# Block transpositions on VectorE and small fetches for retention's v, k and y, with y normalized on ScalarE

## The chip, the cores and the metric
The kernel runs on one core of a Trainium2 chip. A core has several engines, each with its own instruction stream in program order: TensorE (PE in the profile, matmuls), VectorE (DVE), ScalarE (ACT), GpSimd (POOL) and SyncE (SP), which here issues most DMA transfers. Engines wait for one another by semaphores. The metric is the device time of one launch in microseconds (us), lower is better.

## The reference, cut to what matters
One layer: an RMSNorm, an input projection, two groups of heads (retention and windowed attention), a gate, an output projection, a residual and a last RMSNorm. Sequence 1024, model width 2048, all float32.

```python
def hybrid_layer(x, w_in, w_out, norm_w, decay_fwd, decay_bwd, gn_w, gn_b, sink):
    h = rms_norm(x, norm_w)
    proj = h @ w_in                                  # (1024, 2048) @ (2048, 6656)
    rq, rk, rv, rg, aq, ak, av, ag = jnp.split(proj, splits, axis=-1)
    y_ret = retention_branch(rq, rk, rv, decay_fwd, decay_bwd, gn_w, gn_b) * jax.nn.silu(rg)
    y_att = window_attention_branch(aq, ak, av, sink) * jax.nn.silu(ag)
    return x + jnp.concatenate([y_ret, y_att], axis=-1) @ w_out

def retention_chunkwise(q, k, v, log_gamma, include_diag):   # chunks of 128 rows, 8 heads of 128
    scores = jnp.einsum('bhnik,bhnjk->bhnij', qc, kc) * decay
    inner = jnp.einsum('bhnij,bhnjv->bhniv', scores, vc)
    kv_chunk = jnp.einsum('bhnjk,hj,bhnjv->nbhkv', kc, k_dec, vc)
    _, prev = lax.scan(lambda s, kv: (s * chunk_decay + kv, s), zeros, kv_chunk)
    cross = jnp.einsum('bhnik,hi,nbhkv->bhniv', qc, q_dec, prev)
    return inner + cross

# retention_branch: rotary on q and k, the above forwards and backwards, and then per head
y = (y - mean(y)) * lax.rsqrt(var(y) + GN_EPS) * gn_w + gn_b
```

## The kernel before, in words
The two projections are products of 2x2 blocks in seven multiplications instead of eight (operands a11, a12, a21, a22 of the weights and sums of them). Each float32 operand is split into a high and a low part (`split`: ScalarE writes the high part wH at L87, VectorE the low part wL at L84), and a product is three matmuls, L98, L99 and L100 (`mm3`); L100 uses wL. The projected heads go to DRAM as tiles `pr` of 128x1024, with the head's feature in the partition and the position along the row, that is, the transposed form.

The main loop is a clock of steps. In each step TensorE issues two of the projection's products (six matmuls of 128x512), and beside it jobs, written as Python generators, each put a little work of the other stages: the attention's heads, then the eight retention heads, then the gating and the operands of the output projection. `idle(n)` lets n steps pass, `busy` holds the heads whose y isn't finished. The instructions of TensorE, SP and POOL stand in the order in which the jobs write them; those of VectorE and ScalarE are placed by a scheduler.

A retention head takes 28 steps. `fetch` loads kT and qT and their halves for the rotation (`rx`) by SP and rotates them on VectorE (L751, L753, L91); `fetch_v` loads vT by SP (L761). `head` then does, in order: the scores kT x qT (L787), decayed by VectorE into `sd` (L790); `transposed` turns vT into v_tok on TensorE in two bundles of four 128x128 transpositions (L542), which ScalarE copies out (L797), and kT into k_tok likewise (L803); `vd` is v_tok with its decays; the outer products vd x k_tok (L820) give the state of each chunk, which VectorE scans forwards and backwards (L832, L834) and splits into sH and sL, 14 pieces of 128x128; the inner products v_tok x sd (L867) and the cross products with sH, sL give y (L860, L868). `normed` takes statistics of y on VectorE (L882, L883), has POOL raise the variance to the power -1/2 (L888), normalizes y on VectorE in eight instructions (L891), turns it on TensorE (L542) and lets ScalarE scale it by gn_w and gn_b on the way out of PSUM (L899); SP stores it to `mix` (L905), 128x1024 a head.

Of the DMA queues, SP's carries the weights (`a<-in_w_in`, L171; a tile's next load waits until its last reader is done), the heads' loads and the stores of mix, all in one order. In the gating (`operand_tiles`), ScalarE's own queue loads a tile of mix (L1280) and a tile of the gate (L1281), ScalarE applies Silu (L1270) and VectorE multiplies (L1271). In the attention, two tiles of v are turned by `transposed` as well (`take_v`).

## Time and profile before
| what | us |
|---|---|
| median of 3 runs | 1526.39 (1525.41 to 1526.89) |
| span of the profiled execution | 1524.4 |
| its own time beside its span, by the median of the runs | 1526.39 - 1524.4 = 2.0 |
| TensorE busy | 1510.5 |
| VectorE busy | 1088.3 |
| ScalarE busy | 686.6 |
| POOL busy | 151.0 |

The span is the time from the first to the last instruction of one profiled execution. The busy times of the engines overlap, so they don't add up to it; an engine's share says how much of the span it had something running. The profile also has a chain of work that ended last, groups of instructions by line and shape with the mean duration of one, waits with what ended them, DMA transfers with the time from issue to landing, and a timeline. The eight retention heads run from about 690 to 1110 us, the gating of their part from about 1219 to 1284 us.

### The profile page before, as it was taken

The numbers are of one execution on the slowest core, as the hardware profiler recorded it, in microseconds if no ns is written. First come the engines' busy times: TensorE is split into PE (matmuls) and PEld (weight loads), VectorE is DVE, ScalarE is ACT, GpSimd is POOL, SyncE is SP. The second block draws the span as 40 slices with busy tenths as digits, with TensorE's granted clock in tenths as the row PEclk, the third lists the DMA queues.
The fourth block names the chain that finished last, engine by engine and source line by source line (L and its number), as shares of the span: only waits on it lengthen the run. The fifth ranks groups of instructions, "written<-read, shape, count | busy, mean of one in ns | idle before, by whom it ended". The sixth has DMA issues, their size and how long they took to land.

```text
span 1524.4 us, 20497 instructions
## 1 busy us (share of the span) xinstructions
PE 1510.5 (99%) x7406; PEld 1274.0 (84%) x7406; DVE 1088.3 (71%) x1943; ACT 686.6 (45%) x1139; POOL 151.0 (10%) x169
## 2 busy tenths in 40 slices
PE   9999999999999999999999999999999999999997
PEld 7888888788888888888888888888888888888886
DVE  6896594557767575756977797779755966776766
ACT  7543462234545454533445444543444643542425
POOL 0000001111010000011212000001211102020001
PEclk9999999999999999999999999999999999999999
DMA  8288847889573424796677655488689679395756
GB/s 319 68 277 316 311 166 193 222 207 251 163 204 128 138 80 167 281 315 156 139 179 205 196 174 193 152 297 299 157 207 262 152 217 251 85 212 162 219 177 251
DMA packets 153352, 310.53 MB, mean 204 GB/s; under 512 B 13697, under 2 KB 72481, under 8 KB 144418
## 3 DMA queue, kind: packets, MB, share of 16 engines
q1 hardware_dynamic: 128050, 254.15, 49.1%
q0 software_dynamic: 19728, 36.71, 15.6%
q10 hardware_dynamic: 5472, 18.36, 3.5%
q8 instruction: 58, 0.95, 0.3%
q14 instruction: 44, 0.36, 0.1%
HBM read 193.03 MB, written 124.52 MB: 208 GB/s over the span
## 4 chain that ended last, share of the span: by engine, by line
PE 84%; issue 9%; DMA 4%; DVE 2%; POOL 0%; ACT 0%; SPq 0%; ACTq 0%; POOLq 0%; DVEq 0%
PE pj L100 21%; PE pj L98 21%; PE pj L99 21%; PE ax L99 5%; PE ax L100 5%; PE ax L98 5%; PE ax L820 2%; PE ax L542 1%; DMA xt<-in_x_dram 1%; PE ax L619 1%; DMA pr<-ct 1%; PE ax L787 1%; PE ax L867 1%; DMA yt<-pr 1%; DVE wL L84 0%
## 5 line engine op out<-in xcount | busy, mean ns | idle before, releaser
L98 PE MATMUL pj<-c,wH 128*128 128x512 f32 x1444 | 576.8, 399 | 0.0
L100 PE MATMUL pj<-c,wL 128*128 128x512 f32 x1440 | 562.6, 391 | 1.6 <-DVE wL L84 1.6
L99 PE MATMUL pj<-c,wH 128*128 128x512 f32 x1444 | 563.0, 390 | 0.0
L100 PEld LDWEIGHTS pj<-c,wL 128*128 128x128 f32 x1440 | 270.3, 188 | 60.7 <-DVE wL L84 2.5
L98 PEld LDWEIGHTS pj<-c,wH 128*128 128x128 f32 x1444 | 271.6, 188 | 49.7 <-ACT ct L292 0.4
L99 PEld LDWEIGHTS pj<-c,wH 128*128 128x128 f32 x1444 | 271.8, 188 | 49.5 <-DVE c L948 0.2
L87 ACT CAST wH<-a 128x1024 fp32r<-128x1024 f32 (+1 forms) x159 | 166.3, 1046 | 250.2 <-PE pj L99 138.0
L84 DVE TENSOR_TENSOR wL<-a,wH 128x1024 fp32r<-128x1024 f32 x157 | 191.9, 1222 | 109.4 <-ACT wH L87 105.9
L292 ACT COPY ct<-pj 128x512 f32<-128x512 f32 x192 | 111.1, 584 | 220.3 <-PE pj L100 219.7
L262 POOL DMA_DIRECT2D pr<-ct x104 | 92.2, 961 | 612.9 <-DVE ct L91 474.6
L91 DVE TENSOR_TENSOR ct<-pj,ct 128x512 f32<-128x512 f32 x164 | 109.1, 688 | 58.9 <-PE pj L100 58.0
L84 DVE TENSOR_TENSOR wL<-s,wH 128x1024 fp32r<-128x1024 f32 x56 | 68.4, 1222 | 89.8 <-ACT wH L87 89.4
L99 PE MATMUL pj<-wL,c 128*128 128x512 f32 x224 | 87.3, 390 | 0.0
L100 PE MATMUL pj<-wH,c 128*128 128x512 f32 x224 | 87.2, 389 | 0.0
L98 PE MATMUL pj<-wH,c 128*128 128x512 f32 x224 | 87.1, 389 | 0.0
L99 PE MATMUL ax<-wL,c 128*128 128x512 f32 x208 | 81.2, 390 | 0.4 <-DVE wL L84 0.4
L100 PE MATMUL ax<-wH,c 128*128 128x512 f32 x208 | 80.9, 389 | 0.0
L98 PE MATMUL ax<-wH,c 128*128 128x512 f32 x208 | 80.9, 389 | 0.0
L87 ACT CAST wH<-s 128x1024 fp32r<-128x1024 f32 x56 | 59.1, 1055 | 16.4 <-PE ax L100 8.8
L87 ACT CAST sH<-st 128x128 fp32r<-128x128 f32 x112 | 29.9, 298 | 46.9 <-DVE st L834 29.2
L99 PEld LDWEIGHTS pj<-wL,c 128*128 128x128 f32 x224 | 42.0, 188 | 8.9 <-DVE wL L84 0.3
L98 PEld LDWEIGHTS pj<-wH,c 128*128 128x128 f32 x224 | 42.0, 188 | 8.8
(243 smaller groups left out, 2057.7 us busy)
## 6 DMA issues: line engine op xcount, KB each, us to landing
a<-in_w_in_dram SPq DMA_DIRECT2D x103, 512.0 KB, 5.8
kept<-c SPq DMA_DIRECT2D x28, 1024.0 KB, 7.3
c<-kept SPq DMA_DIRECT2D x28, 1024.0 KB, 9.9
pr<-ct SPq DMA_DIRECT2D x110, 256.0 KB, 5.4
pr<-ct POOLq DMA_DIRECT2D x104, 256.0 KB, 6.2
a<-in_w_out_dram SPq DMA_DIRECT2D x18, 512.0 KB, 5.4
rx<-pr SPq DMA_DIRECT2D x64, 128.0 KB, 3.8
ysrc<-mix ACTq DMA_DIRECT2D x16, 512.0 KB, 5.4
```

The source lines that it names most:

```text
L84: return nc.vector.tensor_tensor(out=dst, in0=src, in1=high.bitcast(F32), op=ALU.subtract)
L87: behind(pinned, nc.scalar.copy(out=dst_h, in_=src))
L91: nc.vector.tensor_tensor(out=dst, in0=a, in1=b, op=ALU.add)
L98: nc.tensor.matmul(po, aH, bH, start=first, stop=False, **kw)
L99: nc.tensor.matmul(po, aH, bL, start=False, stop=False, **kw)
L100: nc.tensor.matmul(po, aL, bH, start=False, stop=last, **kw)
L262: nc.gpsimd.dma_start(out=dst, in_=t, accum_op=ALU.add)
L292: nc.scalar.copy(out=t, in_=bank)
L542: nc.tensor.transpose(pt[:, blk(t)], src[:, blk(b * 4 + t)], ident)
L619: nc.tensor.transpose(pt[:, blk(j)], s[:, blk(j)], ident)
L787: nc.tensor.matmul(sc[:, blk(t)], kT[:, c], qT[:, c], start=True, stop=True)
L820: nc.tensor.matmul(p, k_tok[:, c], vd[:, c, d], start=True, stop=True)
```

## The change
VectorE can transpose the 32x32 blocks inside a tile, each block where it stands. If the blocks themselves are moved to their transposed places by a transfer, the two together turn a 128x128 tile. The change does this for v, k and y of the retention heads and for v of the attention; the function `transposed` and its 208 TensorE instructions are gone.

- **v**: `gather` fetches vT from its plain row tile by 16 transfers of 32x8x32 elements (rows of 32 floats, 128 bytes) on SP instead of one; VectorE transposes two halves of 128x512 into v_tok, straight in SBUF. `fetch_v` lets seven steps pass instead of five.
- **k**: when k is rotated, VectorE also transposes its two halves into `ct` tiles, which SP stores to a DRAM tile `kz` in blocks. A new job `fetch_k_tok`, started at the scores, waits until no y is unfinished, and SP fetches k_tok by four transfers of 32x32x32. The next head's kT is started when k_tok is there, instead of before `vd`.
- **y**: a small VectorE instruction makes -mean x rstd; ScalarE normalizes y by eight instructions with scale and bias; VectorE transposes its two halves into `ct`, and SP stores these to mix in blocks. The scale by gn_w and bias by gn_b moves to the gating, as one more ScalarE instruction on each of eight tiles, which are fetched by four transfers on SP instead of one on ScalarE's queue.
- **state splits**: one split for both directions, 128x2x128, seven a head instead of fourteen; sH and sL are laid out by direction, and the cross products read them with a stride.

```diff
+    def gather(q, dst, src):
+        rows = [dst[a * SQ:(a + 1) * SQ] for a in range(P // SQ)]
+        if len(src.shape) == 3:
+            of = src.rearrange("c (b j) (a t) -> a j (c b) t", j=SQ, t=SQ)
+            for a, r in enumerate(rows):
+                q(out=r.rearrange("p (n t) -> p n t", t=SQ), in_=of[a])
+        else:
+            of = src.rearrange("(b j) (c a t) -> a b j c t", j=SQ, t=SQ, a=P // SQ)
+            for a, r in enumerate(rows):
+                r = r.rearrange("p (c b t) -> b p c t", b=P // SQ, t=SQ)
+                for b in range(P // SQ):
+                    q(out=r[b], in_=of[a, b])
...
+                    if c == T_RK:
+                        zs.append(ct())
+                        nc.vector.transpose(out=zs[i], in_=u)
                     yield
                 kq[name, h] = t
+                for i, z in enumerate(zs):
+                    yield
+                    nc.sync.dma_start(out=spot(kz[h], i), in_=chunks(z))
...
-                nc.sync.dma_start(out=t, in_=pr[T_RV + h])
-                yield from idle(5)
+                gather(nc.sync.dma_start, t, pr[T_RV + h])
+                yield from idle(7)
                 vs[h] = t
+
+            def fetch_k_tok(h):
+                while busy:
+                    yield
+                yield
+                t = ret.tile([P, NT, P], F32, name="k_tok", tag="y")
+                gather(nc.sync.dma_start, t.rearrange("p c e -> p (c e)"), kz[h])
+                yield from idle(6)
+                ks[h] = t
...
-                for b, pt in transposed(vs.pop(h)):
-                    nc.scalar.copy(out=v[:, 4 * b:4 * b + 4], in_=chunks(pt))
+                vT = vs.pop(h)
+                for b in range(2):
+                    nc.vector.transpose(out=v[:, 4 * b:4 * b + 4], in_=chunks(vT[:, half(b)]))
                     yield
-                while busy:
-                    yield
-                k_tok = ret.tile([P, NT, P], F32, name="k_tok", tag="y")
-                for b, pt in transposed(kT):
-                    nc.scalar.copy(out=k_tok[:, 4 * b:4 * b + 4], in_=chunks(pt))
-                    yield
-                start(next_of("kT", T_RK, h + 1))
                 vd = ret.tile([P, NT, 2, P], F32, name="vd", tag="vdq")
                 for d in range(2):
                     nc.scalar.mul(vd[:, :, d], v, kd[:, d * RH + h:d * RH + h + 1])
-                yield from idle(3)
+                while h not in ks:
+                    yield
+                k_tok = ks.pop(h)
+                start(next_of("kT", T_RK, h + 1))
...
-                        split(sH[:, 2 * to + d - 1], sL[:, 2 * to + d - 1], cur[:, d])
                         if d == 1:
+                            both = slice(i, 2 * NT - 2 - i, 2 * NT - 3 - 2 * i)
+                            split(sH[:, both], sL[:, both], cur)
                             prev = cur
...
-                for c in range(NT):
-                    nc.vector.tensor_scalar(out=y[:, c], in0=y[:, c], scalar1=mv[:, c, 0:1], scalar2=rs[:, c:c + 1],
-                                            op0=ALU.subtract, op1=ALU.mult)
+                nc.vector.scalar_tensor_tensor(out=mv[:, :, 0], in0=mv[:, :, 0], scalar=-1.0, in1=rs, op0=ALU.mult, op1=ALU.mult)
+                zs = []
+                for b in range(2):
+                    for c in range(4 * b, 4 * b + 4):
+                        nc.scalar.activation(out=y[:, c], in_=y[:, c], func=AF.Identity, scale=rs[:, c:c + 1], bias=mv[:, c, 0:1])
+                    zs.append(ct())
+                    nc.vector.transpose(out=chunks(zs[b]), in_=y[:, 4 * b:4 * b + 4])
+                    yield
+                busy.discard(h)
                 yield from idle(2)
-                outs = []
-                for b, pt in transposed(y.rearrange("p c e -> p (c e)")):
-                    yo = ct()
-                    nc.scalar.activation(out=yo, in_=pt, func=AF.Identity, scale=gw[:, h:h + 1], bias=gb[:, h:h + 1])
-                    outs.append((mix[h][:, half(b)], yo))
-                    yield
-                busy.discard(h)
-                yield
-                for dst, yo in outs:
-                    nc.sync.dma_start(out=dst, in_=yo)
+                for b, z in enumerate(zs):
+                    nc.sync.dma_start(out=spot(mix[h], b), in_=chunks(z))
...
+                if t < RH:
+                    nc.scalar.activation(out=d, in_=d, func=AF.Identity, scale=gw[:, t:t + 1], bias=gb[:, t:t + 1])
                 nc.vector.tensor_tensor(out=d, in0=d, in1=g, op=ALU.mult)
...
-                        behind(True, nc.scalar.dma_start(out=d, in_=mix[t]))
+                        if t < RH:
+                            gather(nc.sync.dma_start, d, mix[t])
+                        else:
+                            behind(True, nc.scalar.dma_start(out=d, in_=mix[t]))
```

Where instructions now stand, at three places. In the changed kernel the same operations have line numbers that are higher by 1 to 36.

SP's queue, from the load of the third retention head's v to the loads for the next k. In the kernel before, the two loads ahead of the stores of mix are a11 and a12 of the next block of weights, and the last row is a22:
```order
L761 DMA vT<-pr_83 128x1024
L171 DMA a_7337<-in_w_in_dram 128x4x256
L1153 DMA res_241<-in_x_dram 16x16384
L171 DMA a_7393<-in_w_in_dram 128x4x256
L171 DMA a_7395<-in_w_in_dram 128x4x256
L905 DMA mix_118<-ct 128x512 x2
L738 DMA kT<-pr_76 128x1024
L744 DMA rx<-pr_76 64x512 x4
L171 DMA a_7514<-in_w_in_dram 128x4x256
```
And in the changed kernel (a_7364 is a21, a_7416 and a_7418 are a11 and a12, a_7502 is a22):
```order
L163 DMA vT<-pr_83 32x8x32 x16
L782 DMA kz_135<-ct 128x4x128 x2
L194 DMA a_7364<-in_w_in_dram 128x4x256
L936 DMA mix_118<-ct 128x4x128 x2
L1184 DMA res_249<-in_x_dram 16x16384
L194 DMA a_7416<-in_w_in_dram 128x4x256
L194 DMA a_7418<-in_w_in_dram 128x4x256
L157 DMA k_tok<-kz_135 32x32x32 x4
L194 DMA a_7502<-in_w_in_dram 128x4x256
L758 DMA kT<-pr_76 128x1024
L764 DMA rx<-pr_76 64x512 x4
```
The stores of mix stand ahead of a11 and a12, k_tok's four transfers have taken the place behind them, and kT stands behind k_tok and a22, where it stood ahead of a22. Each of SP's transfers here also waits, in the built program, for the one that was issued eight transfers before it.

VectorE in the same stretch, behind the second head's y, from the variance on. Before (a_6849 is a21, a_6904 a11, a_6906 a12, a_7025 a22; wL is the low part of the operand behind it):
```order
L887 TENSOR_SCALAR rstd<-mv 128x8
L91 TENSOR_TENSOR a_6849<-a_6849,a_7025 128x1024
L91 TENSOR_TENSOR ct<-pj,ct 128x512 x2
L891 TENSOR_SCALAR y<-y,mv,rstd 128x128 x4
L84 TENSOR_TENSOR wL<-a_6849,wH 128x1024
L753 TENSOR_TENSOR rx<-rx,rot 128x512
L891 TENSOR_SCALAR y<-y,mv,rstd 128x128
L91 TENSOR_TENSOR qT<-qT,rx 128x512
L891 TENSOR_SCALAR y<-y,mv,rstd 128x128 x3
L94 TENSOR_TENSOR s_7191<-a_6906,s_7191 128x1024
L84 TENSOR_TENSOR wL<-a_6904,wH 128x1024
```
Now, from the row behind rstd's (a_6896 is a21, a_6949 a12, a_7033 a22; the row with mv is the new small instruction, which needs POOL's result):
```order
L773 TENSOR_TENSOR rx<-rx,rot 128x512
L771 TENSOR_TENSOR qT<-qT,rot 128x512
L92 TENSOR_TENSOR qT<-qT,rx 128x512
L925 SCALAR_TENSOR_TENSOR mv<-mv,rstd 128x8
L773 TENSOR_TENSOR rx<-rx,rot 128x512
L92 TENSOR_TENSOR ct<-pj,ct 128x512 x2
L931 STREAM_TRANSPOSE ct<-y 128x512
L92 TENSOR_TENSOR qT<-qT,rx 128x512
L92 TENSOR_TENSOR a_6896<-a_6896,a_7033 128x1024
L931 STREAM_TRANSPOSE ct<-y 128x512
L95 TENSOR_TENSOR s_7203<-a_6949,s_7203 128x1024
L85 TENSOR_TENSOR wL<-a_6896,wH 128x1024
```
The normalization of y is gone from VectorE, two transpositions of y have come, and wL of a21, which stood behind four of the eight normalizations, stands behind both transpositions and the update of s.

VectorE at the start of a state scan, one head earlier. Before:
```order
L751 TENSOR_TENSOR kT<-kT,rot 128x512
L91 TENSOR_TENSOR ct<-pj,ct 128x512 x2
L84 TENSOR_TENSOR wL<-a_6538,wH 128x1024
L832 COPY st<-ax 128x128 x2
L834 SCALAR_TENSOR_TENSOR st<-st,cd,ax 128x128
L84 TENSOR_TENSOR sL<-st,sH 128x128 x2
L834 SCALAR_TENSOR_TENSOR st<-st,cd,ax 128x128
L84 TENSOR_TENSOR sL<-st,sH 128x128
L753 TENSOR_TENSOR rx<-rx,rot 128x512
L84 TENSOR_TENSOR sL<-st,sH 128x128
L834 SCALAR_TENSOR_TENSOR st<-st,cd,ax 128x128 x2
```
Now:
```order
L85 TENSOR_TENSOR wL<-a_6566,wH 128x1024
L866 COPY st<-ax 128x128 x2
L868 SCALAR_TENSOR_TENSOR st<-st,cd,ax 128x128 x2
L85 TENSOR_TENSOR sL<-st,sH 128x2x128
L771 TENSOR_TENSOR kT<-kT,rot 128x512
L85 TENSOR_TENSOR sL<-st,sH 128x2x128
L771 TENSOR_TENSOR kT<-kT,rot 128x512
L868 SCALAR_TENSOR_TENSOR st<-st,cd,ax 128x128 x2
L773 TENSOR_TENSOR rx<-rx,rot 128x512
L85 TENSOR_TENSOR sL<-st,sH 128x2x128
L868 SCALAR_TENSOR_TENSOR st<-st,cd,ax 128x128 x2
L92 TENSOR_TENSOR kT<-kT,rx 128x512
```
The first rotation step of k for the next head stood ahead of wL and the scan; now both such steps stand behind the first split of the scan, with the rest of the scan behind them.

More of the change, by code (lines that the diff above doesn't have):

```diff
@@ L19 @@
 P = 128
+SQ = 32
 S = 1024
@@ L535, in rotate_att @@
         return rotate(pool, rot_a, [([(c, 0, 32) for c in tiles], [(c, r, 16) for c in tiles for r in (16, 0)]) for tiles in sets])
-    def transposed(src):
-        for b in range(2):
-            pt = ax()
-            for t in range(4):
-                nc.tensor.transpose(pt[:, blk(t)], src[:, blk(b * 4 + t)], ident)
-            yield b, pt
     clock = [0]
@@ L566, in fetch @@
                 kv[n] = att.tile([P, S], F32, name="ld", bufs=2)
-                nc.sync.dma_start(out=kv[n], in_=pr[c])
+                if n == "ldv":
+                    gather(nc.sync.dma_start, kv[n], pr[c])
+                else:
+                    nc.sync.dma_start(out=kv[n], in_=pr[c])
             def take_k():
@@ L574, in take_v @@
                 kv["v"] = vH, vL = [att.tile([P, NT, P], F32R, name="v" + c) for c in "HL"]
-                for b, pt in transposed(kv["ldv"]):
-                    split(vH[:, 4 * b:4 * b + 4], vL[:, 4 * b:4 * b + 4], chunks(pt))
+                for b in range(2):
+                    z = ct()
+                    nc.vector.transpose(out=z, in_=kv["ldv"][:, half(b)])
+                    split(vH[:, 4 * b:4 * b + 4], vL[:, 4 * b:4 * b + 4], chunks(z))
                     yield
@@ L792, in head @@
                     sds.append(sd)
+                start(fetch_k_tok(h))
                 while h not in vs:
```

22 lines of the change are left out of this document (14 added, 8 removed).

## The prediction
> **What bounds the kernel now.** I read the page first: its head, its engines, its DMA queues and the chain that ended last.
> ```profile
> span 1524.4 us, 20497 instructions
> ...
> PE 1510.5 (99%) x7406; PEld 1274.0 (84%) x7406; DVE 1088.3 (71%) x1943; ACT 686.6 (45%) x1139; POOL 151.0 (10%) x169
> ...
> q1 hardware_dynamic: 128050, 254.15, 49.1%
> ...
> q10 hardware_dynamic: 5472, 18.36, 3.5%
> ...
> PE 84%; issue 9%; DMA 4%; DVE 2%; POOL 0%; ACT 0%; SPq 0%; ACTq 0%; POOLq 0%; DVEq 0%
> ```
> TensorE is busy 99% of the span and carries 84% of the chain. So every microsecond taken from TensorE comes off the end, and every microsecond that it is made to wait goes on. The other engines matter only through the few instructions that TensorE waits for. The span is 1524.4 us; the median of the runs is 1526.39, so 2.0 us lie around the span, and I add them at the end.
>
> **What leaves TensorE.** "Busy" does not say what a transposition costs there, since matmuls overlap. The timeline of TensorE in the first head does:
> ```profile
> 709.50 0.39 PE L100 MATMUL pj<-c,wL 128*128 128x512 f32 x1
> ...
> 710.18 0.39 PE L100 MATMUL pj<-c,wL 128*128 128x512 f32 x1
> 710.41 0.60 PE L542 MATMUL ax<-ident,vT 128*128 128x128 f32 x4
> ...
> 711.30 0.39 PE L100 MATMUL pj<-c,wL 128*128 128x512 f32 x1
> ```
> From one L100 to the next is 0.68 us without transpositions (709.50 to 710.18) and 1.12 with four (710.18 to 711.30). A bundle of four costs 0.44 us. The groups by line and shape give the count:
> ```profile
> L542 PE MATMUL ax<-ident,y 128*128 128x128 f32 x64 | 9.6, 272 | 0.0
> L542 PE MATMUL ax<-ident,vT 128*128 128x128 f32 x64 | 9.6, 272 | 0.0
> L542 PE MATMUL ax<-ident,kT 128*128 128x128 f32 x64 | 9.6, 272 | 0.0
> L542 PE MATMUL ax<-ident,ld 128*128 128x128 f32 x16 | 2.4, 271 | 0.0
> ```
> All 208 go, 52 bundles: 52 x 0.44 = **22.9 us off**. The other matmuls stay, in the same order. Everything below is what of this comes back as waits of TensorE, taken in the head that runs from 721.8 us, and then by the number of heads.
>
> **The engines that take the work over.**
> ```profile
> L91 DVE TENSOR_TENSOR ct<-pj,ct 128x512 f32<-128x512 f32 x164 | 109.1, 688 | 58.9 <-PE pj L100 58.0
> ...
> L891 DVE TENSOR_SCALAR y<-y,mv,rstd 128x128 f32<-128x128 f32 x64 | 18.4, 342 | 5.0 <-POOL rstd L888 5.0
> ...
> L87 ACT CAST sH<-st 128x128 fp32r<-128x128 f32 x112 | 29.9, 298 | 46.9 <-DVE st L834 29.2
> ```
> The busy times of one head (TensorE, its weight loads, VectorE, ScalarE, POOL):
> ```profile
> 743.00:794.00 51.00, 51.00 (x282) 43.92 (x281) 41.19 (x101) 22.93 (x41) 9.67 (x9) 1.00 0.68 159
> ```
> VectorE gets six 128x512 block transpositions a head, which the trace does not show. The nearest rows are L91 at 0.69 us for the same tile (0.6 between starts) and, as bounds, 0.34 (L891, a quarter of the elements) and 1.22 (twice the elements, rows below); I take 0.6, as the shape is the same. The eight normalizations that leave took 0.26 each between starts, 2.1 us, so VectorE's sum rises by 6 x 0.6 - 2.1 = 1.5 us a head and falls by about 0.5 through the merged state splits: it has 10 of 51 us free there. ScalarE gives up six evictions and takes eight short operations (near L87's 0.30): less work; the scaling of eight tiles that moves to the gating falls among its waits there. Both sums are covered; the order of the work is what can cost.
>
> The Trainium skill, "VectorE: DVE Perf Modes", section "The three transpose paths", gives 390 ns on TensorE and 311 ns on VectorE for a 128x128 bf16 tile, and only 32x32 blocks on VectorE. As an estimate from it, a 128x512 call would take 1.24 us instead of 0.6; no run here shows it. On TensorE the trace has 272 ns for one, and 0.11 of time lost by it, so that page's 390 is not what leaving TensorE saves here.
>
> **Term 1: y's chain.** First the outer products (L820), the scores (L787) and y on TensorE, then VectorE around y:
> ```profile
> 721.82 1.06 PE L820 MATMUL ax<-vd,k_tok 128*128 128x128 f32 x8
> 755.94 1.05 PE L787 MATMUL ax<-qT,kT 128*128 128x128 f32 x8
> 756.84 0.60 PE L542 MATMUL ax<-ident,y 128*128 128x128 f32 x4
> 758.65 1.06 PE L787 MATMUL ax<-qT,kT 128*128 128x128 f32 x8
> ```
> ```profile
> 740.85 1.53 DVE L860 SCALAR_TENSOR_TENSOR y<-ax,qd,y 128x128 f32<-128x128 f32 x4
> ...
> 749.32 0.19 DVE L887 TENSOR_SCALAR rstd<-mv 128x8 f32<-128x8 f32 x1
> ...
> 752.20 1.12 DVE L891 TENSOR_SCALAR y<-y,mv,rstd 128x128 f32<-128x128 f32 x4 [0.36 <-POOL rstd L888]
> 753.23 1.22 DVE L84 TENSOR_TENSOR wL<-a,wH 128x1024 fp32r<-128x1024 f32 x1
> ```
> Before, wL of a21 is ready at 754.45. In the changed order the work from the first y to rstd sums to the same 8.5 us (740.85 to 749.32; s and one k transposition in, three rotation steps out), so rstd stays at 749.3 and POOL's answer at 752.2. But now the small multiply that waits for POOL stands ahead of: one rx (0.57), two ct (1.2), the first ct<-y (0.6), qT (0.6), a (1.13), the second ct<-y (0.6), s (1.13) and wL (1.22). That is 7.1 us: ready at 759.3. TensorE needs it at the third matmul behind the second scores: 758.65 less the bundle of y at 756.84, plus 0.90 for the scores (755.94 to 756.84) and 0.45, 759.55. So over 5 us of slack become 0.2. With transpositions at 1.22, three on this way, it is 1.7 late; at 0.34 it is 1.0 early. The rest of that queue (scores' decay, v's transpositions, the next wL) waits with it. I put 0.3 us a head in seven heads: **+2.1 us** (0 to 12).
>
> **Term 2: k_tok.** SP and VectorE in the same head, and landings by DMA group:
> ```profile
> 743.81 0.34 SPq L761 DMA_DIRECT2D vT<-pr  x1
> 754.48 5.43 SPq L171 DMA_DIRECT2D a<-in_w_in_dram  x3
> ...
> 767.47 0.32 SPq L738 DMA_DIRECT2D kT<-pr  x1
> 767.84 2.37 SPq L744 DMA_DIRECT2D rx<-pr  x4
> ```
> ```profile
> a<-in_w_in_dram SPq DMA_DIRECT2D x103, 512.0 KB, 5.8
> ...
> rx<-pr SPq DMA_DIRECT2D x64, 128.0 KB, 3.8
> ...
> kT<-pr SPq DMA_DIRECT2D x8, 512.0 KB, 3.9
> vT<-pr SPq DMA_DIRECT2D x8, 512.0 KB, 6.0
> ...
> rx<-pr SPq DMA_DIRECT2D x40, 32.0 KB, 3.9
> ```
> The four fetches of k_tok (128 KB each) stand behind a11 and a12, which wait for the wL behind term 1's: 759.3 + 0.6 (decay) + 0.6 (v) + 1.2 = 761.7. Two issues of 0.4 (0.34 at 743.81) and four of 0.44 (a quarter of the 2.37 at 767.84 is 0.59 with its waits) end at 764.3. Landing takes 3.8 us (rx of that size) to 5.8 (a, ahead of it in the queue): 768.1 to 770.1. The outer products come 48 matmuls of 0.227 behind the scores' end: 758.2 + 0.9 + 10.9 = 770.0. So it just fits, until packets cost more: each gather is 4096 packets of 128 bytes, 256 an engine. Of the page's queues, q10 gives 156 ns a packet of 3.4 KB (3.5% of 16 x 1524 us over 5472), q1 94 ns at 2.0 KB; the line through both gives 10 ns at 128 bytes, 94 is the other end. So 2.6 to 24 us of each engine; I take 16 ns, near the line, 4 us against the 1.5 that 512 KB in long rows cost. I put 0.75 us a head in eight: **+6 us** (0 to 24).
>
> **Term 3: kT.** It moves behind k_tok and a22: the wL that frees a22 ends 1.2 us after the outer products start (row below, 772.70), so kT is issued 1.6 after instead of 5.3 before, and lands at 5.5 by its median. In four of the heads VectorE's order has both rotation steps of k directly behind the first state pairs, so it idles from about 2.9 to 5.5, with state splits queued behind, for which the cross products wait.
> ```profile
> 772.70 1.22 DVE L84 TENSOR_TENSOR wL<-a,wH 128x1024 fp32r<-128x1024 f32 x1
> ...
> 786.62 1.23 DVE L84 TENSOR_TENSOR wL<-a,wH 128x1024 fp32r<-128x1024 f32 x1 [0.89 <-ACT wH L87]
> 787.76 0.49 DVE L84 TENSOR_TENSOR sL<-st,sH 128x128 fp32r<-128x128 f32 x2
> ```
> Before, the last split ends 788.25, 15.5 behind the outer products, 0.4 ahead of its use; with 0.9 idle to recover and 0.5 from the merged splits, 2.6 - 1.8 = 0.8 is left: 4 x 0.8 = **+3.2 us** (0 to 16, kT's landings reach 11.2).
>
> **Term 4: v and the gating.** v's 16 fetches of 32 KB have eight in flight; at 0.44 each and 3.9 to land, the last is there 11.7 us after 743.8, at 755.5, and VectorE wants it at 759.9: nothing. The attention's two fetches likewise. In the gating, these are the packets from 1219 to 1283 us, and the longest wait of the chain there:
> ```profile
> DMA packets 6123, 15.66 MB, mean 245 GB/s; under 512 B 544, under 2 KB 544, under 8 KB 6120
> ```
> ```profile
> 1264.24 10.67 DMA yt<-pr
> ```
> and the weight load of TensorE that came late through it:
> ```profile
> 1280.83 0.19 PEld L99 LDWEIGHTS ax<-wL,c 128*128 128x128 f32 x1 [0.87 <-DVE wL L84]
> ```
> The eight tiles add 31,700 packets to 6,123, 2.6 to 5 us of every engine for a tile, while ScalarE waits for yt in order and the operand behind it is already 0.87 us late once. The last use lies 15 us behind the last tile, so most is hidden: **+2 us** (-0.9 to +10).
>
> **Sum.** 1524.4 - 22.9 + 2.1 + 6 + 3.2 + 2 = 1514.8; with 2.0 around it **1516.8 us**.
>
> **The rivals.** *All waits hidden:* every estimate is one or two us from zero, and ScalarE is freer; 1524.4 - 22.9 + 2.0 = 1503.5, 1502.6 if the gating's 0.87 goes too. *The gain given back:* terms 1 and 2 at twice my price (+8.1) and 1.5 us more in the gating: 1526.4, for which the slack of 0.2 us in term 1 speaks, and against it that TensorE has next to no waits now. *Slower, through v's queue:* the sixteenth fetch lands 2 x l + 3.9 us behind the first issue, l being the landing of one. Above l = 6.1 v holds up VectorE at its transposition, behind it the wL that frees a11, behind that k_tok: 2 us a head for each us of l, sixteen in all. At l = 6.7 nothing is left of the gain, at 6.9 it is slower by over 0.2%, at 7.2 the time is 1534. For it: vT's own landings, 6.0 and up to 10.4; against it: 3.9 for pieces of 32 KB. *That the change does not do what it says* would need bundles that cost nothing; the timeline speaks against it.
>
> By the Trainium skill, "DMA: Bandwidth & Descriptors", section "Specifications", moves under 512 bytes are below line rate and are done as read-modify-write. By that rule the gathers cost more than the line through the queues says, and the slow case, 1534, is the likelier one; the trace cannot tell, as only 544 of the 6,123 packets of the gating's row are that short.
>
> **How the numbers follow.** All hidden 0.22, my forecast (1508 to 1523) 0.48, gain given back 0.14, slower 0.16. 0.2%, about 3 us, is what a measurement of this kernel can tell from no change: below 1523.3 is faster, above 1529.4 slower. The given-back case counts as same but for 0.02 of its chance. Range: from the hidden case to where half of the slow one lies, 1503 to 1531.
>
> **What would show it.** The changed profile should have no transpositions of y, v and k on TensorE, and some 13 us of idle time or late starts on it. Right or wrong by step: wL of a21 named as releaser of TensorE before the outer products (term 1); the outer products waiting for DMA k_tok (term 2); the cross products waiting for sL, with VectorE's kT waiting for DMA (term 3); TensorE's idle time around 1260 to 1290 (term 4); block transpositions far from 0.6 us. Waits of VectorE's v_tok on DMA vT would be the slow case. My forecast is wrong if TensorE waits under 5 us or over 20 in all.

## The result, and the profile after
The changed kernel takes 1604.8 us (1603.68 to 1607.02), the kernel before on the same chip 1526.11 (1525.41 to 1526.89): a ratio of 1.0519 [1.0504, 1.0534]. It is 5% slower where 0.6% faster was predicted. The page's head, engines, packets, main queue and chain, as shown of before:
```profile
span 1601.8 us, 20324 instructions
...
PE 1517.0 (95%) x7198; PEld 1273.0 (79%) x7198; DVE 1103.0 (69%) x1883; ACT 684.9 (43%) x1107; POOL 148.2 (9%) x169
...
DMA packets 275432, 318.92 MB, mean 199 GB/s; under 512 B 123745, under 2 KB 198913, under 8 KB 266498
...
q1 hardware_dynamic: 251282, 266.75, 53.0%
...
PE 67%; issue 10%; DMA 9%; SPq 6%; DVE 6%; ACT 1%; POOL 0%; DVEq 0%; ACTq 0%; POOLq 0%
```
TensorE has lost its 208 transpositions (7406 to 7198) but its share fell from 99% to 95%, and in the chain from 84% to 67%; DMA and SP's queue took the place. TensorE's longest waits (line, releaser: total, times, longest):
```profile
PE ax L854 <- DMA k_tok<-kz: 43.8, 8, 12.4
PE pj L99 <- ACT wH L88: 8.1, 2, 6.2
PE pj L99 <- DVE ct L1448: 6.4, 1, 6.4
PE ax L99 <- ACT qbH L88: 5.7, 1, 5.7
```
The first is k_tok, in all eight heads; the second and third lie in the gating, the fourth in the attention. All of TensorE's waits come to some 75 us, where the prediction named more than 20 as its own sign of being wrong. Laying the 6,372 three-part matmuls of both traces side by side by their count gives the loss by stage, from their start times:

| up to matmul | before, us | after, us | difference | so this stage |
|---|---|---|---|---|
| 3000, attention done | 692.2 | 699.0 | +6.8 | +6.8 |
| 5300, retention done | 1270.9 | 1326.6 | +55.7 | +48.9 |
| 5500, gating done | 1317.0 | 1394.9 | +77.9 | +22.2 |
| span | 1524.4 | 1601.8 | +77.4 | -0.5 |

Matmul 5300 lies well behind the heads: at 1095 us of the kernel before, in the last head, the difference is already +56.7. With the 22.9 us of bundles that did leave (at the prediction's price), 100.3 us came back. In the third head, this is what SP issues (start, how long the issues take, count):
```profile
812.52 11.18 SPq L163 DMA_DIRECT2D vT<-pr  x16
823.80 1.16 SPq L782 DMA_DIRECT2D kz<-ct  x2
827.62 0.37 SPq L194 DMA_DIRECT2D a<-in_w_in_dram  x1
828.04 1.08 SPq L936 DMA_DIRECT2D mix<-ct  x2
829.17 0.68 SPq L1184 DMA_DIRECT2D res<-in_x_dram  x1
829.95 1.73 SPq L194 DMA_DIRECT2D a<-in_w_in_dram  x2
831.77 10.05 SPq L157 DMA_DIRECT2D k_tok<-kz  x4
```
Four issues of k_tok take 10.05 us here (6.4 to 10.1 over the eight heads). The chain of the same stretch shows which, and the timeline of TensorE what it cost:
```profile
831.77 0.54 SPq L157
832.35 5.01 SPq L157
837.41 3.47 SPq L157
840.92 6.39 DMA k_tok<-kz
```
```profile
847.45 2.05 PE L854 MATMUL ax<-vd,k_tok 128*128 128x128 f32 x8 [8.54 <-DMA k_tok<-kz]
849.15 0.78 PE L99 MATMUL pj<-c,wH 128*128 128x512 f32 x1
...
851.34 0.39 PE L101 MATMUL pj<-c,wL 128*128 128x512 f32 x1
851.57 1.05 PE L854 MATMUL ax<-vd,k_tok 128*128 128x128 f32 x8
852.38 0.48 PE L99 MATMUL pj<-c,wH 128*128 128x512 f32 x1
```
TensorE waits 8.54 us, from 838.91. Then it also runs slowly: the eight outer products take 1.70 us to the next start (847.45 to 849.15) where the next eight take 0.81 (851.57 to 852.38), and the five matmuls behind them 2.19 (849.15 to 851.34) where five starts 0.227 apart take 1.14. That is 0.9 + 1.05, some 2 us more for this wait. Why is seen in the stretches of 4 us (busy times by engine, then the granted clock of TensorE, then the load of the DMA engines, above 1 where packets overlap):
```profile
844.00:848.00 4.00, 0.55 (x2) 0.58 (x3) 0.00 (x0) 0.00 (x0) 0.00 (x0) 0.50 1.14 287
848.00:852.00 4.00, 4.00 (x17) 3.53 (x17) 2.02 (x7) 0.81 (x2) 0.00 (x0) 0.60 1.37 432
852.00:856.00 4.00, 4.00 (x26) 3.53 (x25) 4.00 (x12) 0.81 (x2) 0.00 (x0) 1.00 0.06 21
```
The clock was at 0.50 when k_tok came, and by the trace's record of the clock it was back at 1.00 from 851.2 on, which makes the 0.60 of the stretch to 852. Over the whole trace TensorE's waits are some 71 us longer than before. The other 29 of the 100.3 are nearly all this: during 56 us of its work the record has the clock at 0.50 (the program's end left out), and half of that is 28.

The third head is not like all the others. In the first seven the first issue comes 7.6 to 4.5 us before TensorE needs k_tok; in the last it comes when TensorE already stands, behind reloads of the operand c that stand ahead of k_tok in the last two heads alone, and the wait is the longest of all:
```profile
1113.74 3.20 SPq L1140 DMA_DIRECT2D c<-kept  x1
1116.99 10.08 SPq L157 DMA_DIRECT2D k_tok<-kz  x4
```
```profile
1129.34 2.04 PE L854 MATMUL ax<-vd,k_tok 128*128 128x128 f32 x8 [12.39 <-DMA k_tok<-kz]
```

### The profile page after: what moved, and what is told of

It is laid out like the page before. It is cut to its first block, busy times and chain, and to the rows that moved or that the text cites. A ratio compares the mean times of both kernels' runs of the same rounds, so it can differ in the third digit from the quotient of the medians.

```text
span 1601.8 us, 20324 instructions
## 1 busy us (share of the span) xinstructions
PE 1517.0 (95%) x7198; PEld 1273.0 (79%) x7198; DVE 1103.0 (69%) x1883; ACT 684.9 (43%) x1107; POOL 148.2 (9%) x169
## 4 chain that ended last, share of the span: by engine, by line
PE 67%; issue 10%; DMA 9%; SPq 6%; DVE 6%; ACT 1%; POOL 0%; DVEq 0%; ACTq 0%; POOLq 0%
PE pj L99 17%; PE pj L101 17%; PE pj L100 17%; PE ax L101 4%; PE ax L99 4%; PE ax L100 4%; SPq L157 4%; DMA k_tok<-kz 2%; PE ax L854 2%; DMA xt<-in_x_dram 1%; PE ax L639 1%; DVE wL L85 1%; DMA kT<-pr 1%; SPq L163 1%; DMA pr<-ct 1%
## 5 line engine op out<-in xcount | busy, mean ns | idle before, releaser
L101 PEld LDWEIGHTS pj<-c,wL 128*128 128x128 f32 x1440 | 273.9, 190 | 62.8 <-DVE wL L85 4.2
L99 PEld LDWEIGHTS pj<-c,wH 128*128 128x128 f32 x1444 | 275.4, 191 | 51.5
L100 PEld LDWEIGHTS pj<-c,wH 128*128 128x128 f32 x1444 | 275.1, 191 | 51.6 <-DVE c L979 0.2
L99 PE MATMUL pj<-wH,c 128*128 128x512 f32 x224 | 89.5, 399 | 14.5 <-ACT wH L88 8.1
L101 PE MATMUL pj<-wH,c 128*128 128x512 f32 x224 | 88.8, 397 | 0.0
L854 PE MATMUL ax<-vd,k_tok 128*128 128x128 f32 x224 | 38.1, 321 | 43.8 <-DMA k_tok<-kz 43.8
L854 PEld LDWEIGHTS ax<-vd,k_tok 128*128 128x128 f32 x224 | 36.5, 233 | 49.4 <-issue 44.7
L88 ACT CAST sH<-st 128x256 fp32r<-128x256 f32 x56 | 22.7, 406 | 108.6 <-DVE st L868 55.1
L88 ACT CAST wH<-s 128x1024 fp32r<-128x1024 f32 x56 | 58.9, 1053 | 23.2 <-DVE s L95 11.6
```

Source lines behind the costliest of these rows:

```text
L88: behind(pinned, nc.scalar.copy(out=dst_h, in_=src))
L99: nc.tensor.matmul(po, aH, bH, start=first, stop=False, **kw)
L100: nc.tensor.matmul(po, aH, bL, start=False, stop=False, **kw)
L101: nc.tensor.matmul(po, aL, bH, start=False, stop=last, **kw)
L854: nc.tensor.matmul(p, k_tok[:, c], vd[:, c, d], start=True, stop=True)
```

## The experiments
All times are beside the kernel before on the same chip, 1525.8 to 1526.8 us. Edits are against the changed kernel where nothing else is said. Nine versions, those without an interval behind their time, were executed once. The theory was that k's way through DRAM costs most of it, the gating and the attention's fetches the rest; the rivals were that v's many fetches or VectorE's new order do it.

**k_back**: k by TensorE again, with the next head's kT started where it was before; all else as changed. Its main lines:
```diff
-                while h not in ks:
-                    yield
-                k_tok = ks.pop(h)
+                k_tok = ret.tile([P, NT, P], F32, name="k_tok", tag="y")
+                for b, pt in transposed(kT):
+                    nc.scalar.copy(out=k_tok[:, 4 * b:4 * b + 4], in_=chunks(pt))
...
```


> The change with k alone taken back: k_tok is turned on TensorE again, kz and its short fetches are gone; v, y and the gating stay changed. Theory A (SP's queue takes only so many short rows at a time, and k_tok stands where TensorE has 11 us for it): the 46.9 us of gaps before the outer products go and with them some 16 us at half clock, 16 bundles of 0.44 come back: 1604.8 - 46.9 - 16 + 7 = about 1549. Theory B (the 106,500 short packets load the DMA engines, wherever they stand): k's 32,768 are 31% of them, 31% of the 101 us lost goes: 1604.8 - 31 + 7 = about 1581.

1550.73 us, as theory A had it: 54 of the 79 us go with k's way through DRAM and the late kT. TensorE's longest waits that are left:
```profile
PE pj L99 <- ACT wH L88: 10.6, 2, 10.4
PE ax L99 <- ACT qbH L88: 5.6, 1, 5.6
PE ax L828 <- issue: 4.2, 1, 4.2
```
They lie in the gating, in the attention and in the last head; heads one to seven, with v's sixteen fetches and the new order of y still in them, show none of over 1 us. So v does not hold the heads up.

**y_back**: y is normalized on VectorE and turned on TensorE again, mix has plain rows, the gating is as before.


> The change with y alone taken back: y is normalized on VectorE, turned on TensorE, and the gating fetches plain rows on ScalarE's queue; v and k stay changed. Theory A: the 22 us lost in the gating go, 16 bundles (7 us) come back, and k_tok's gaps stay: about 1590, with over 40 us of gaps before the outer products. Theory B: 31% of the loss goes, and gaps before the outer products shrink as well: about 1581.

1584.7 us, between the two numbers. The gating's loss is gone (+1.0 where it was +22.2), as theory A had it, and k_tok's waits shrank as well, as theory B had it:
```profile
PE ax L862 <- DMA k_tok<-kz: 19.5, 6, 10.9
```
So part of k_tok's wait hangs on y. In the first five heads the fetch of k_tok now starts 7.3 to 10.6 us before it is needed, where it was 5.6 to 7.6. In the changed kernel y's blocked stores stand ahead of k_tok in SP's order, which could explain it; this run alone does not show it. This run also got a new wait of 12.2 us on a reload of the operand c, whose cause stays open.

**kz_scatter**: the short rows on the store of k instead of its fetch: 32 transfers of 16 KB a head in, one of plain rows out.
```diff
-                    nc.sync.dma_start(out=spot(kz[h], i), in_=chunks(z))
+                    scatter(nc.sync.dma_start, kz[h], i, z)
...
-                gather(nc.sync.dma_start, t.rearrange("p c e -> p (c e)"), kz[h])
+                nc.sync.dma_start(out=t.rearrange("p c e -> p (c e)"), in_=kz[h])
```


> The change with k's short rows moved from the fetch to the store: 32 transfers a head write kz in rows of 128 bytes right behind v's fetches, and k_tok comes by one transfer of 4 KB rows in its old place. As many short packets as in the change. Theory A: the outer products no longer wait for k_tok, some 60 us less, though a21 now stands behind the 32 stores on SP: 1545 to 1575. Theory B: no change, about 1605.

1682.27 us, which neither theory had. SP's row and TensorE's wait:
```profile
837.16 16.70 SPq L154 DMA_DIRECT2D kz<-ct  x32
```
```profile
PE ax L862 <- DMA k_tok<-kz: 131.2, 8, 23.6
```
The 32 transfers hold SP for 16.70 us, 0.52 for each 16 KB, waits included, and what stands behind them comes later: the fetch of k_tok starts 4.0 to 15.3 us after TensorE needs it, in all eight heads. The number of transfers on an in-order queue is a price of its own.

**k_512**: rows of 512 bytes instead of 128. VectorE writes the blocks with the position inside a group of four innermost, a fetch has 256 rows instead of 1,024, and TensorE reads k_tok with a stride of four.
```diff
-                        nc.vector.transpose(out=zs[i], in_=u)
+                        nc.vector.transpose(out=zs[i].rearrange("p (a t c) -> p c a t", c=4, t=SQ),
+                                            in_=u.rearrange("p (c a t) -> p c a t", c=4, t=SQ))
...
-                        nc.tensor.matmul(p, k_tok[:, c], vd[:, c, d], start=True, stop=True)
+                        nc.tensor.matmul(p, k_tok[:, c // 4, c % 4], vd[:, c, d], start=True, stop=True)
```


> The change with k's short rows made four times as long: VectorE writes the transposed blocks with the position in the group of four chunks innermost, so kz is stored in plain rows and k_tok is fetched in the same four transfers of the same bytes, but in rows of 512 instead of 128 bytes (1,024 rows a head instead of 4,096). Place and order stay. Theory A1 (SP can't issue on while too many rows are outstanding; the second and third of the four issues took 2 to 5 us in each head): issues near 0.6 us, gaps before the outer products from 46.9 to under 10 us, about 1550. Theory A2 (k_tok is only the last of a queue of bytes: stores of mix, a11, a12): gaps stay above 30 us, about 1590.

1610.84 us, no gain, and above the numbers of both theories. In the place of the 10.05 us above SP has:
```profile
828.20 3.65 SPq L799 DMA_DIRECT2D k_tok<-kz  x4
```
So it is the rows that hold SP in a fetch of k_tok, as the count of transfers is the same. But the waits fell to 34.8 us only, theory A2's sign. SP is done with the four issues 2.1 to 4.6 us after it starts them, where the changed kernel took 6.4 to 10.1, and yet the outer products start 7.9 to 14.0 us behind the first issue, where they started 9.0 to 15.7 behind it. So the long issue is not most of what makes k_tok late. A second price came in as well, the weight loads of the outer products:
```profile
L856 PEld LDWEIGHTS ax<-vd,k_tok 128*128 128x128 f32 x224 | 55.2, 325 | 40.7 <-issue 37.6 <-ACT wH L88 1.4
```

**k_stride** measures that price by itself: the kernel before, with k_tok laid out for the same stride and nothing else changed.


> The kernel before, with one thing of k_512 alone: k_tok lies in SBUF with a stride of four floats along a chunk's features (ScalarE writes it so), and TensorE loads it as weights with that stride. In k_512 the outer products' weight loads took 325 ns instead of 191 and their matmuls 397 instead of 275. If the stride alone does that: 224 x 0.12 to 0.13 = 27 to 30 us more, about 1554, and k_512's time holds that much that has nothing to do with rows. If it was the wait for k_tok: no change, 1526.

1549.47 us, 23.5 more than before, a little under the 27 to 30 expected. Its row, and that of the kernel before:
```profile
L820 PEld LDWEIGHTS ax<-vd,k_tok 128*128 128x128 f32 x224 | 54.6, 323 | 1.4
```
```profile
L820 PEld LDWEIGHTS ax<-vd,k_tok 128*128 128x128 f32 x224 | 30.0, 191 | 2.8
```
By their starts the outer products now follow each other in 0.233 us instead of 0.112; 192 such steps are 23.2 us. As an estimate, k_512 without this would be near 1587, close to theory A2's 1590.

**k_early** starts the fetch of k_tok as the first thing in a head, ahead of a21, a11 and a12; **k_early_512** does that with the 512-byte rows.
```diff
                 kT, qT = kq.pop(("kT", h)), kq.pop(("qT", h))
+                start(fetch_k_tok(h))
...
-                start(fetch_k_tok(h))
                 while h not in vs:
```


> The change with k_tok's four fetches started two steps earlier, ahead of a21, a11 and a12 on SP's queue; rows of 128 bytes as in the change. Theory A1: the issues still take 2 to 3 us each, but begin some 5 us earlier: gaps before the outer products 10 to 25 us, 1560 to 1580. Theory A2: with 1.5 MB less ahead nothing is left of the gaps: about 1545. If the weights that now stand behind are late instead, TensorE waits for wH or wL in the heads.

> The change with both: rows of 512 bytes for k, as in k_512, and k_tok's fetches ahead of a21, a11 and a12, as in k_early. Either alone left 33 to 39 us of gaps before the outer products. Theory C (what is ahead of k_tok on the DMA engines and its own 4,096 rows both have to fit into the 5 us that y's chain leaves): with 1,024 rows and nothing but mix's stores ahead, the last lands about 4 us behind the first issue, gaps under 8 us in all; against the change some 45 us and the half clock behind them are saved: 1604.8 - 39 - 14 = about 1550. Against it (the landing is late for another reason): gaps of 25 us or more, 1580 or above.

1583.06 and 1589.01 us (1565 or so for the second without its strided loads, an estimate by k_stride). Waits on k_tok: 30.4 us, 7 times, and 22.0, 6 times. The first is just outside theory A1's ranges, and theory C's 1550 is missed. Both parts help, and both together don't suffice: k_tok shares its buffer with y, so its fetch can't start before y's last transposition has read it. In k_early's third head that transposition ends at 816.60, the fetch starts at 819.01, and TensorE stands from 824.50, so the place in SP's order bought no earlier start.

**k_two_queues**: two of the four fetches go to ScalarE's queue.
```diff
-                gather(nc.sync.dma_start, t.rearrange("p c e -> p (c e)"), kz[h])
+                for a in range(P // SQ):
+                    (nc.scalar if a % 2 else nc.sync).dma_start(...)
```


> The change with k_tok's four fetches shared out: two stay on SP's queue, two go to ScalarE's; rows of 128 bytes. Theory A1 (the room is each queue's own): no issue above 1 us on ScalarE, gaps before the outer products halved or less, 1560 to 1575. Theory A2: the DMA engines have the same work ahead, gaps of 40 us or more, about 1600.

1612.87 us; k_tok's waits 38.9 instead of 43.8, others grew by more. ScalarE's two fetches hold their queue for 0.31 to 0.98 us each, as theory A1 had it, but those whose landing the trace tells land 3.6 to 10.0 us after their issue, and the waits stay, as theory A2 had it. So room on SP's queue is not all that k_tok lacks.

**att_back**: the attention's v by TensorE and one plain fetch each again.


> The change with the attention's v taken back: two plain fetches and four bundles on TensorE. The trace of the change shows q's load issued behind the 16 small fetches and landing 8 us later, with TensorE waiting 5.7 us for it and half a clock behind. Expected: 8.7 us less between 434 and 456 us, 1.8 more for the bundles, all else as in the change: 1604.8 - 7 = about 1598. If the small fetches aren't the cause, 1606.

1598.52 us, as expected: 6.3 less than the changed kernel's median and 5.2 less than its lowest. Where the table has +6.8 for the attention, this trace has -0.1.

**all_512**: 512-byte rows for k and for y, k early, the attention as before.


> A version of the change with its short rows made longer where that can be done: k in rows of 512 bytes and ahead of the weights (k_early_512), y's blocks stored in plain rows and fetched in rows of 512 bytes in the gating (the gate's tile takes the place of mix's and the product is written in order by VectorE in two halves), the attention's v as before; retention's v as in the change. 48 bundles stay off TensorE (21.1 us). If theory C holds for the gating too, its 22 us shrink to under 5; some gaps before the cross products and in the last head stay (8 to 12 us with the half clock): 1526.3 - 21.1 + 5 + 12 = about 1522. If the gating is slow for the place of its fetches on SP, not for their rows: about 1540.

1567.41 us, a ratio of 1.0272 [1.0255, 1.0289], far above the 1522 expected. The gating lost 2.4 us instead of 22.2, with the same four transfers a tile on SP, so there the rows were most of it (the tile's place and VectorE's product in two halves changed with them); k_tok's waits (21.6 us) and the strided weight loads remain.

**v_alone** adds only retention's v to the kernel before; **v_0_6** the same without the last head.
```diff
-                nc.sync.dma_start(out=t, in_=pr[T_RV + h])
+                gather(nc.sync.dma_start, t, pr[T_RV + h])
...
-                for b, pt in transposed(vs.pop(h)):
-                    nc.scalar.copy(out=v[:, 4 * b:4 * b + 4], in_=chunks(pt))
+                vT = vs.pop(h)
+                for b in range(2):
+                    nc.vector.transpose(out=v[:, 4 * b:4 * b + 4], in_=chunks(vT[:, half(b)]))
```


> The kernel before with retention's v alone by 16 small fetches and VectorE; k, y, the attention and the gating as before. Theory A: nothing waits for v, 16 bundles leave TensorE: 1526.1 - 7.0 = about 1519. Theory B: 31% of the loss with 7 us off: about 1550. The slow rival of the prediction (v holds up VectorE): above 1526.

> The kernel before with v of the first seven retention heads by small fetches and VectorE; the last head, in which v_alone lost 7 us, turns v on TensorE as before. 14 bundles less: 1526.3 - 6.2 = 1520.1 if nothing else moves, 1524 if the 3.9 us that v_alone lost in the gating come again.

1530.21 us, 1.003 [1.002, 1.004], and 1527.61, 1.0012 [1.0002, 1.0021]: both miss what theory A and the 14 bundles promised. v_alone's time is the slow rival's, but its mechanism isn't seen: no wait of VectorE there is put down to vT. Up to the seventh head v_alone gains 7.2 us, where 14 bundles of 0.44 are 6.2. Then one wait before the last head's scores gives it back: 3.2 us in both, and the half clock behind it. In v_alone a wait of 2.0 us for a wL costs some 3 more in the gating. In the trace of v_0_6 the rotation of q for that head stands behind a wL in VectorE's order, so the miss suggests that the head in which it shows isn't the head whose v causes it; vy_0_5 bears that out.

**y_512** is the kernel before with y alone by VectorE, 512-byte rows, and the change's merged state splits; **vy_512** adds v in the first seven heads; **vy_0_5** in the first six.
```diff
-                if h < RH - 1:
+                if h < RH - 2:
```


> The kernel before with y's part alone, in long rows: y normalized on ScalarE, turned by VectorE, stored in plain rows, fetched for the gating in rows of 512 bytes; k and v (the attention's too) turned on TensorE as before; the state splits merged as in the change. 16 bundles less: 1526 - 7 + 1 to 3 for the gating = 1520 to 1522. If y's chain on VectorE makes wL late in each head (term 1 of the prediction, 0.5 to 1 us), 1524 to 1527.

> y_512 and v_0_6 together: y in long rows, and v of the first seven heads by small fetches. 30 bundles less: 1526 - 13.2 + 1 to 3 for the gating + the 5 that v_0_6 lost in the last head = 1518 to 1521. If the two together bring new waits in the heads (SP's queue behind v, VectorE's behind y), 1525 or more.

> vy_512 with v by small fetches in the first six heads only. In vy_512 TensorE stood 4.35 us before the last head's scores, for which VectorE's rotation of q came late; y_512, without v's fetches, has no such gap. If the fetches of the seventh head's v cause it: 4.4 and the half clock behind it (about 1) less, two bundles (0.9) more: 1524.1 - 4.5 = about 1519.5. If it is not them, 1525.

1526.36 us, 1.0 [0.9989, 1.001]; 1524.06, 0.9986 [0.9978, 0.9995]; 1519.6, **0.9954 [0.994, 0.9968]**. y alone gains 3.7 us up to the gating (of 7.0 by the price of its 16 bundles) and loses 5.5 there in the profiled execution. vy_512 missed its 1518 to 1521 by a wait of 4.0 us before the last head's scores. With v in six heads nothing waits there, as was expected if the seventh head's fetches cause it, and this version beats both kernels:
```profile
span 1517.8 us, 20348 instructions
...
PE 1500.8 (99%) x7294; PEld 1262.9 (83%) x7294; DVE 1088.2 (72%) x1867; ACT 694.0 (46%) x1127; POOL 149.7 (10%) x169
```
It leaves 112 transpositions out (7406 to 7294), 28 bundles or 12.3 us by the prediction's price; the time falls by 6.7. What the merged state splits give of this was not measured apart; their new layout costs TensorE nothing that shows, as the cross products with 256 columns take 291 and 282 ns on average in y_512 as they did before.

**Not tried:** a buffer of its own for k_tok, so that its fetch could go out as soon as k is stored. There is no room for it beside the other tiles. Whether k could then pay is open.

## Why the prediction was wrong, by its own steps
- **What leaves TensorE, 22.9 us: held for v, and for v and y together, but not for y alone.** Up to 1059 us of the kernel before, v_alone gains 7.2 us for 14 bundles (6.2 by the price) and vy_512 11.1 for 26 to 28 (11.4 to 12.3). y_512 gains only 1.9 there for 12 to 14 bundles, and 1.5 us of waits for wL explain only part of what is missing.
- **Term 2, k_tok, failed: +6 put, some 60 measured.** In the changed kernel's trace that is 43.8 of waits and, by the record of the clock, 15.6 lost at half clock behind the eight; k_back gives 54 back and does without 7.0 of k's own bundles (16 x 0.44), 61, with term 3 in it. The step that failed is the time from the first issue to the last landing. It was put at four issues of 0.44 and 3.8 to 5.8 us behind them, 5.6 to 7.6; in the third head it took 15.5 (831.77 to 840.92 + 6.39), and over the eight heads the outer products start 9.0 to 15.7 us behind the first issue. The issues took 6.4 to 10.1 us instead of 1.8, as the rows of before from which the 0.44 came are of far fewer rows of data each; k_512 shows that this goes with the rows, and also that short issues alone bring only a little. The packets on the engines ahead (y's two stores, res, a11, a12) were in the order and were not added up; how much of the wait is theirs was not measured apart, and stays open. The price of a packet was right: 15 ns on average for the 128-byte packets of this trace, 16 taken.
- **Term 2's start held in most heads and failed in the last.** The prediction's times gave 7.5 us from the first issue to the need. The third head has 7.1 (831.77 to 838.91), the seventh 4.5 and the last none, and these last two make 20.1 of the 43.8 us of waits. One head times eight left out that the last two have reloads of c in SP's queue. The term's end of 24 us for all eight heads, 3 a head, also doesn't fit its own dearest packet, which was reckoned as 24 us of every engine in one head.
- **Term 4: v right, attention and gating wrong.** VectorE stood 1.1 us in all before v_tok, and no wait of TensorE is put down to it. In the third head SP issues the sixteen fetches in 11.18 us and the last lands 14.2 us after the first issue; 11.7 was put, and VectorE did not wait for it there. The attention, put at nothing, cost 8.6 us: the table's 6.8 and the 1.8 of its own four bundles. The step "the attention's two fetches likewise" looked at v alone and not at what is queued behind it. The chain there:
```profile
436.21 0.64 SPq L163
436.85 0.04 issue
436.90 0.65 SPq L602
437.55 0.04 issue
437.60 7.64 DMA q<-pr
...
445.31 0.41 ACT qbH L88
445.73 0.04 issue
445.77 0.58 PE ax L99
```

q's load (L602) stands behind the small fetches, and TensorE behind q. The gating, put at 2 with 10 as its end, cost 22. On SP, the fetches of a tile of mix
```profile
1271.76 16.85 SPq L157 DMA_DIRECT2D ysrc<-mix  x12
...
1298.34 10.12 SPq L157 DMA_DIRECT2D ysrc<-mix  x4
...
1309.12 8.86 SPq L157 DMA_DIRECT2D ysrc<-mix  x4
```

take SP 5.6 to 10.1 us for four (the last three tiles 6.5, 8.4 and 8.1), waits for yt among them, where "2.6 to 5 us of every engine" was reckoned and the time of issue was left out. With rows of 512 bytes in all_512 four take 2.3 to 6.7, and the loss is nearly gone.
- **Terms 1 and 3 stayed inside their bounds.** VectorE's block transposition of 128x512 takes 0.70 us (0.6 between starts, as taken), ScalarE's scaling 0.48 where 0.30 was the nearest row:
```profile
L931 DVE STREAM_TRANSPOSE ct<-y 128x512 f32<-128x512 f32 x16 | 11.3, 708 | 1.4 <-ACT y L929 1.4
```
```profile
L929 ACT ACTIVATE y<-y,mv,rstd 128x128 f32<-128x128 f32 x64 | 25.6, 482 | 33.3 <-DVE mv L925 33.3
```

No wait of size on wL of a21 came of it: the heads of the changed kernel have one of 0.9 us on a wL, those of k_back none. Term 3's mechanism shows: VectorE waits for kT in six heads, 14.8 us in all, in the second head
```profile
792.82 0.69 DVE L771 TENSOR_TENSOR kT<-kT,rot 128x512 f32<-128x512 f32 x1 [6.11 <-DMA kT<-pr]
```
and the cross products wait in two heads, in gaps of 0.7 to 1.1 us, 4.1 together against the 3.2 put. The clock fell behind both rows of gaps, 4.8 us more; 9 is inside the term's 0 to 16.
- **The slow rival had the right sign and the wrong mechanism.** It went through v's queue, and TensorE never waited for v. The rule weighed beside it goes the right way: by the Trainium skill, "DMA: Bandwidth & Descriptors", section "Specifications", moves under 512 bytes are below line rate. A packet of 128 bytes takes 15 ns in the changed kernel's trace; one of 512 takes 27 there, where nearly all of them are stores, and 39 in all_512, where they are the longer fetches. So a byte of a fetch costs 1.5 times as much in the short rows; the gating's 22 us became 2.4 with the long ones. For k_tok long rows alone did not mend it.
- **What no step had:** what a wait costs beyond itself. All terms took a wait of x us as x; the half clock behind the waits came to 28 us.

## What to carry to other kernels
A transposition that costs 0.44 us a bundle in a full stream of TensorE is cheap, and what replaces it must be on time every time, in the odd last head too: add up the issues of a fetch, everything ahead of it on its queue and on the DMA engines, and its own rows, from the moment that its buffer is free, and compare that with the time until it is needed. Price each transfer on an in-order queue for those behind it as well, q behind v here. Where part of a change waits, try the parts apart: 28 of these 52 bundles, with y in longer rows, were worth 6.7 us, where all of them cost 79.

## What the runs showed of the hardware
- **SP is held by fetches of many rows in a row.** Of the four fetches of 1,024 rows of 128 bytes, the first three took SP 0.54, 5.01 and 3.47 us in the third head, and in all eight heads the second and third took 1.64 to 5.39; fetches of 256 rows of 512 bytes, the same 128 KB, 0.91 each there (3.65 / 4). What SP waits for in the long ones was not measured. Waits included, a transfer of 16 KB costs SP 0.52 us in kz_scatter, one of 32 KB 0.70 (11.18 / 16).
- **A wait of some 2 us can cost TensorE its clock, and need not.** In the trace of after the granted clock fell to 0.5 thirteen times before the end: behind eleven single waits, the shortest of 1.88 us, and behind two rows of gaps of 0.7 to 1.1 us each in the cross products. Single gaps up to 1.0 us left it alone, there and in before. Each fall lasts 3.41 us or a multiple of it in the trace's record of the clock, 85 us in all, waits included. The falls also start on a grid of 3.41 us (728.35 to 782.96 is 16 of them), so it matters how a wait lies on it. The first wait for k_tok, 725.50 to 727.37, lies inside the stretch from 724.94 to 728.35, at whose end the clock falls. One of the same 1.88 us in the gating, 1341.24 to 1343.12, lies across the line at 1342.74 and left the clock alone until a wait of 6.4 us came behind it. Waits of 2.1 us in k_early and y_back and of 2.2 us in k_two_queues left it alone as well; what share of a stretch it takes was not measured. The Trainium skill, "TensorE: Matmul & The Clock Gate", section "HAM oscillation — how this bites in real kernels", tells of a window of 3.4 us and of waits longer than it; the length agrees, but a wait of little over half of it was enough here.
- **A stationary operand with a stride of four floats** loads in 323 ns instead of 191, and 224 outer products take 23.5 us longer (k_stride, one execution).
- **VectorE turns the 32x32 blocks of 128x512 floats in 0.70 us,** about what an addition of that size takes (L91, 0.69). The estimate of 1.24 worked out from the Trainium skill, "VectorE: DVE Perf Modes", section "The three transpose paths", does not hold for this form.
